# Two chunks of a projection by eight plain products instead of seven Winograd products, in an encoder block on one core

## The chip, the core and the metric

The kernel runs on one core of a Trainium2 chip. The core has a matrix engine (PE, with a loader for the stationary operand, PEld), three engines for elementwise work (DVE, ACT and POOL) and SP, which here only issues transfers. Each engine takes its instructions strictly in the order in which the program holds them, and waits for semaphores that other engines and transfers raise. The metric is device time in microseconds from the first to the last instruction of the one core; the median of three runs of the kernel before is 1972.98 us (1972.03 to 1973.51).

## What is computed

One layer of an encoder. `x` has 2048 rows of 1024 features. All that matters here stands at the head of the reference:

```python
h = rms_norm(x, norm_gain[l])
proj = jnp.einsum('bsd,df->bsf', h, w_in[l])
q_a, k_a, v_a, g_a, q_r, k_r, v_r, g_r, m_a, m_r = split_columns(proj)
# chunk_band_attention on q_a, k_a, v_a; retention_chunkwise on q_r, k_r, v_r;
# both gated, projected, merged, projected by w_out, added to x, normalised
```

Inputs and outputs are float32, and a float32 product is made of three passes: every operand is held as a high part (rounded to the engine's format) and a low part (what the rounding left), and high x high, low x high and high x low are summed.

## The kernel before

**Tiling.** The rows come in two passes of 1024 (`s` = 0, 1). In a pass the normalised rows, transposed, are a 2 x 2 matrix of blocks: a11 and a12 are the left and right 512 features of the first 512 rows (`xa` in the code), a21 and a22 those of the next 512 (`xb`). The weights come in chunks of 256 columns, and a chunk is also 2 x 2: b11, b12 (upper features, left and right 128 columns), b21, b22 (lower features). Job `p0` is the first pass over 14 chunks: chunk 0 is q of the attention, chunk 1 its k, chunk 2 the k of the retention (which is then rotated), and so on. After it come the gates (`g0`), the second pass (`p1`, `g1`), and the output projections, with attention and retention woven in between.

**Seven products.** A chunk is made by the Winograd form of Strassen's method (class `Strassen`, L334): seven products instead of eight, of operands that are sums. On the side of the rows seven operands lie resident in R[0] to R[6], as high and low parts: R[0] = a11, R[1] = a12, R[2] = a22, R[3] = s1 = a21 + a22, R[4] = s2 = s1 - a11, R[5] = s3 = a21 - a11, R[6] = s4 = a12 - s2. On the side of the weights POOL makes four differences per chunk, t1 to t4 (`SUMS_OF`, L320, and `sum`, L335; at which product they are made stands in `SUM_AT`, L321). `PRODUCTS` (L227) pairs them; `ORDERS` (L44) gives the order of the seven by the first letter of the job. Each operand of the weights is split by ACT (`wh`, the high part) and DVE (`wl`, the low part) in `make`, L294. The results u2, u3 and c22 are summed by ACT and DVE out of PSUM in `product`, L372, before an epilogue (`ep_qa`, `ep_ka`) splits them again and stores them by SP.

**A product** is 12 matmuls of 128x512 on PE (`matmuls`, L302: four slices of 128 features, three passes), counted as four steps. `run_to(n)` (L529) emits steps until the n-th; `prime(n)` (L457) emits the preparation of the weights for the first n products; `later` puts a piece of work some steps on.

**The front.** At the start nothing is resident. `start_up` (L545) writes out an order by hand: SP loads the rows and the eight quarters of the weights of chunks 0 and 1; ACT and DVE sum the squares and scale the rows; PE transposes them (16 transposes of 128x128 for each of the four blocks, into four PSUM buffers `TR`); `hi` (ACT) and `lo` (DVE) split the transposed blocks into R, `to_parts` the sums. The products of the two chunks stand in between, in the order `FRONT` (L45), by turns for chunk 0 and chunk 1: with R[0], R[1], R[2], R[4], R[5], R[3], R[6]. From chunk 2 on the order "p" holds, and `dense` (L468) emits the products with the preparation three products ahead. `keep_in_program_order` makes every engine keep the order in which the code is written, so an instruction that waits holds back all that stands behind it on its engine.

## Time and profile before

| what | value |
|---|---|
| median of 3 runs | 1972.98 us (1972.03 to 1973.51) |
| the profiled execution: its time, its span | 1975.88 us, 1974.2 us |
| PE busy, share of the span | 1906.4 us, 97% |
| DVE, ACT, POOL busy | 71%, 48%, 50% |
| PE busy in 17 to 32, 32 to 47, 47 to 58, 58 to 70 us | 14.86 of 15, 11.21 of 15, 7.58 of 11, 8.69 of 12 us |
| first matmul of a product; first of chunk 2; first of chunk 3 | 17.16, 78.45, 97.49 us |

How to read it: a row of the timeline gives start, duration, engine, line, operation, the tile written and the tiles read by the program's names without their numbers, the shape, the count of merged instructions, and in brackets how long the engine sat idle just before and what ended that. Nearly all instructions have line 142, where the helper records them, so the tiles tell them apart: `r` is a part of R, `wh_p` and `wl_p` are parts of weights in job p0 or p1, `t_p` a difference of weights, `pa` and `p` are PSUM tiles of transposed rows, `ps_p_x`, `y`, `v`, `z`, `w` the PSUM banks of the Winograd products, `raw_f` and `b` the weights of chunks 0 and 1, `raw_p` those of later chunks. A matmul's duration runs on into the next one, so the step of PE is read from start to start.

### The profile page before, as it was taken

What the parts mean: (1) busy time and instruction counts of PE and PEld (TensorE: products, weight loads), DVE (VectorE), ACT (ScalarE), POOL (GpSimd) and SP (SyncE); (2) the same over time, 40 slices, a digit from 0 to 9 for tenths busy, and PEclk for the clock granted to TensorE, in tenths of its full rate; (3) what the DMA queues carried; (4) which work ended last, traced back from release to release, by engine and by line L of the source; (5) the groups of instructions that cost most, each with busy time, mean ns of one, the idle gap of its engine ahead of it and who ended that gap; (6) DMA issues with size and microseconds to landing.
All of it is one profiled execution on the core that took longest, in us unless ns stands there. A gap on an engine that the chain in (4) does not pass through costs nothing. (4 is left out here: it accounts for less than half of the span.)

```text
span 1974.2 us, 30273 instructions
## 1 busy us (share of the span) xinstructions
PE 1906.4 (97%) x9616; PEld 1586.6 (80%) x9616; DVE 1399.1 (71%) x2567; ACT 938.7 (48%) x1893; POOL 993.1 (50%) x799
## 2 busy tenths in 40 slices
PE   6899999999999999999999999999999999999997
PEld 4677878888888887778887888888888878887886
DVE  7887778677765667988887677766556754557876
ACT  6454554466655454433343555554456322223554
POOL 2343544554556666544544454444566214557775
PEclk9999999999999999999999999999999999999999
DMA  4575796655539996676684745553999899987674
GB/s 150 165 259 183 228 297 207 205 162 170 174 113 283 272 269 234 209 246 196 192 256 161 211 141 163 165 162 102 273 278 296 294 371 332 313 271 244 202 222 142
DMA packets 335054, 434.84 MB, mean 220 GB/s; under 512 B 30040, under 2 KB 194544, under 8 KB 334896
## 3 DMA queue, kind: packets, MB, share of 16 engines
q1 hardware_dynamic: 269152, 368.42, 58.8%
q10 hardware_dynamic: 65744, 64.50, 10.7%
q8 instruction: 77, 1.26, 0.3%
q14 instruction: 81, 0.66, 0.1%
HBM read 288.21 MB, written 144.60 MB: 219 GB/s over the span
## 5 line engine op out<-in xcount | busy, mean ns | idle before, releaser
L142 POOL TENSOR_SCALAR pr<-pr,rsum 128x640 f32<-128x640 f32 (+4 forms) x128 | 96.0, 750 | 226.6 <-DVE ptl L142 108.3
L142 POOL TENSOR_TENSOR t_p<-raw_p,t_p 128x512 f32<-128x512 f32 x50 | 74.2, 1484 | 148.8 <-DVE wl_p L142 131.1
L142 PE MATMUL ps_p_z<-r,wh_p 128*128 128x512 f32 x448 | 141.4, 397 | 5.5 <-DVE c_p L142 2.8
L142 PE MATMUL ps_g_z<-r,wh_g 128*128 128x512 f32 x448 | 144.2, 403 | 2.0 <-DVE c_g L142 1.9
L142 DVE CUSTOM_DVE_ANT_0 pr<-wide,bt 128x640 f32<-128x640 f32 (+4 forms) x128 | 94.3, 737 | 71.6 <-PE wide L142 62.5
L142 PE MATMUL ps_g_x<-r,wh_g 128*128 128x512 f32 x448 | 142.9, 400 | 0.7 <-ACT u_g L142 0.7
L142 PE MATMUL ps_p_x<-r,wh_p 128*128 128x512 f32 x448 | 141.7, 397 | 1.4 <-ACT u_p L142 1.4
L142 ACT ACTIVATE pr<-pr,mn 128x640 f32<-128x640 f32 (+4 forms) x128 | 98.0, 765 | 84.9 <-DVE mn L142 84.9
L142 DVE TENSOR_TENSOR ptl<-tp,pth 128x384 fp32r<-128x384 f32 x168 | 95.9, 573 | 41.1 <-ACT pth L142 40.6
L142 ACT CAST pth<-tp 128x384 fp32r<-128x384 f32 x168 | 84.6, 515 | 70.9 <-PE tp L142 65.3
L142 POOL TENSOR_TENSOR sl<-sm,sh 128x512 fp32r<-128x512 f32 x64 | 89.4, 1397 | 57.3 <-ACT sh L142 30.9
L142 DVE TENSOR_TENSOR wl_p<-t_p,wh_p 128x512 fp32r<-128x512 f32 x112 | 105.9, 947 | 1.9 <-ACT wh_p L142 1.9
L142 DVE TENSOR_TENSOR sm<-sr,dm 128x512 f32<-128x512 f32 x64 | 44.1, 689 | 79.1 <-PE sr L142 35.2
L142 PEld LDWEIGHTS ps_p_z<-r,wh_p 128*128 128x128 f32 x448 | 81.7, 188 | 22.7 <-issue 5.5
L142 PEld LDWEIGHTS ps_p_x<-r,wh_p 128*128 128x128 f32 x448 | 83.4, 190 | 19.7 <-ACT u_p L142 2.2
L142 PE MATMUL wide<-ka,qa 128*128 128x512 f32 (+2 forms) x448 | 94.7, 327 | 2.3 <-DVE mn L142 2.3
L142 POOL TENSOR_TENSOR wl_g<-t_g,wh_g 128x512 fp32r<-128x512 f32 x56 | 75.3, 1345 | 41.4 <-ACT wh_g L142 31.4
L142 PEld LDWEIGHTS tp<-ident,pr 128*128 128x128 f32 x560 | 71.3, 141 | 27.5 <-POOL pr L142 2.2
L142 PE MATMUL po<-pth,va 128*128 128x256 f32 x336 | 92.8, 297 | 0.0
L142 ACT CAST wh_p<-t_p 128x512 fp32r<-128x512 f32 x112 | 69.1, 619 | 49.0 <-PE ps_p_z L142 22.5
L142 PE MATMUL tp<-ident,pr 128*128 128x128 f32 x560 | 89.0, 273 | 2.9 <-POOL pr L142 1.6
L142 PEld LDWEIGHTS wide<-ka,qa 128*128 128x128 f32 x448 | 75.5, 189 | 19.5 <-DVE mn L142 7.7
(885 smaller groups left out, 6023.7 us busy)
## 6 DMA issues: line engine op xcount, KB each, us to landing
raw_g<-in_w_in_dram ACTq DMA_DIRECT2D x56, 512.0 KB, 5.3
raw_p<-in_w_in_dram ACTq DMA_DIRECT2D x50, 512.0 KB, 6.1
qa<-qas SPq DMA_DIRECT2D x128, 128.0 KB, 3.0
qr<-qrs SPq DMA_DIRECT2D x128, 128.0 KB, 4.7
vr<-vrs SPq DMA_DIRECT2D x64, 256.0 KB, 5.6
ka<-kas SPq DMA_DIRECT2D x40, 256.0 KB, 3.7
va<-vas SPq DMA_DIRECT2D x40, 256.0 KB, 3.1
kds<-kdt_k SPq DMA_DIRECT2D x32, 256.0 KB, 4.8
```

Of the source, the lines that this page charges most:

```text
L142: return tc.keep_in_program_order(op(*a, **k))
```

## The change

Chunks 0 and 1 of job p0 are made by the eight plain products a(i,j) x b(j,h), class `Front`, without t1 to t4 and without u2, u3 and c22: the two products with j = 0 and j = 1 add up in one PSUM bank, and the epilogue reads the bank. The order is i, then j, then the chunk, then h: the first eight products need only a11 and a12, the next four a21, the last four a22. a21 is held in R[6] until the twelfth product is done, and the parts of the weights, which are used twice, lie in R[5] (b11, b12) and R[3] (b21, b22) until the twelfth and the sixteenth. Sums s1 to s4 are made beside the products; s4 = a12 - s2 goes from DVE to POOL. The third chunk uses order "h": R[0], R[2], R[4], R[5], R[3], R[1], R[6], with t1, t2, t3 made before its first product and t4 before its second. The loads of the weights' quarters stand earlier on SP, between the rows of the first and the second block, and the loads of chunk 2 earlier on ACT. `second_half`, which prepares the second pass, is given 8 steps instead of 24, counted from a place that is 24 steps later.

```diff
-FRONT = (0, 3, 5, 1, 2, 4, 6)
+ORDERS["h"] = (0, 5, 1, 2, 4, 3, 6)
...
+        "h": {0: ("t1", "t2", "t3"), 5: ("t4",)},
...
+    class Front(Chunk):
+        def prepare(self, n):
+            i, j, c = n
+            if i:
+                return
+            m, slot = (5, 3)[j], 2 * self.c + c
+            ws = [R[m][part][:, slot, :].rearrange("p (k c) -> p k c", k=4) for part in range(2)]
+            src = self.b[f"b{j + 1}{c + 1}"]
+            act.copy(ws[0], src)
+            dve.tensor_tensor(ws[1], src, r32(ws[0]), ALU.subtract)
+            self.parts[j, c] = ws
+        def product(self, n):
+            i, j, c = n
+            o = self.bank((i, c))
+            yield from self.matmuls(o, self.parts[j, c], R[((0, 1), (6, 2))[i][j]], j == 0, j == 1)
+            if j:
+                self.job.epilogue(self.c, i, c, o, True)
...
+            kind = lambda c: Plain if resident else Front if name == "p0" and c < front else Strassen
...
+            if name == "p0":
+                self.orders[front] = "h"
...
+                seq[:0] = [(c, n) for n in LAST for c in range(front)] if name == "p1" else [
+                    (c, (i, j, h)) for i in range(2) for j in range(2) for c in range(front) for h in range(2)
+                ]
...
         prime(2)
+        run_to(4)
         a11 = [E(f"a11_{k}") for k in range(4)]
...
-        run_to(4)
-        prime(3)
+        prime(4)
+        run_to(8)
         ps = [TR(f"pa1_{k}") for k in range(4)]
...
+        run_to(16)
+        for f in (0, 1):
+            for t in range(4):
+                scale(xb, "b", t, f, t % 2)
+        prime(8)
...
+        run_to(24)
+        ps = [TR(f"p21_{k}") for k in range(4)]
...
+            hi(6, k, ps[k], k)
+            lo(6, k, ps[k], k)
+            if k == 1:
+                run_to(28)
+        run_to(32)
...
+        for k in range(4):
+            dve.scalar_tensor_tensor(s2[k], ps[k], ng[:, 4 + k:5 + k], s3[k], ALU.mult, ALU.add)
+            pool.tensor_tensor(s4[k], a12[k], s2[k], ALU.subtract)
...
-    second_half(24)
+    second_half(8)
```

**On PE, at the start.** `pa` with a number are the transposed rows, `ps_p_0_x` the first bank of chunk 0; `r_81` and `r_82` are the parts of R[0], `r_91` and `r_92` of R[5]. Before, behind the last matmuls of the first product:

```order
L142 MATMUL ps_p_0_x<-r_81,wh_p_0_0_537 128x512
L142 MATMUL ps_p_0_x<-r_82,wh_p_0_0_537 128x512
L142 MATMUL ps_p_0_x<-r_81,wl_p_0_0_538 128x512
L142 MATMUL pa_0_608<-ident,xa_1_454 128x128
L142 MATMUL pa_0_608<-ident,xa_1_456 128x128
```

and with the change:

```order
L142 MATMUL ps_p_0_(0, 0)_586<-r_81,r_91 128x512
L142 MATMUL ps_p_0_(0, 0)_586<-r_82,r_91 128x512
L142 MATMUL ps_p_0_(0, 0)_586<-r_81,r_92 128x512
L142 MATMUL ps_p_0_(0, 1)_611<-r_81,r_91 128x512
L142 MATMUL ps_p_0_(0, 1)_611<-r_82,r_91 128x512
```

A second product with R[0] now stands ahead of the transposes of the right half of `xa`.

**On POOL, its first work.** `t_p_0`, `t_p_1` and `t_p_2` are the differences of weights of chunks 0, 1 and 2, `a_0_672` to `a_3_675` the tiles of a12, `a_0_599` to `a_3_602` those of s2. Before:

```order
L142 TENSOR_TENSOR t_p_0_717<-raw_f_471 128x512
L142 TENSOR_TENSOR t_p_0_719<-raw_f_472,t_p_0_717 128x512
L142 TENSOR_TENSOR t_p_0_721<-raw_f_472,t_p_0_719 128x512
L142 TENSOR_TENSOR t_p_1_800<-raw_f_473 128x512
L142 TENSOR_TENSOR t_p_1_802<-b_641,t_p_1_800 128x512
L142 TENSOR_TENSOR t_p_1_804<-b_640,t_p_1_802 128x512
L142 TENSOR_TENSOR t_p_0_865<-raw_f_471,raw_f_472 128x512
L142 TENSOR_TENSOR t_p_1_867<-raw_f_473,b_641 128x512
```

and with the change:

```order
L142 TENSOR_TENSOR a_0_672<-a_0_672,a_0_599 128x512
L142 TENSOR_TENSOR a_1_673<-a_1_673,a_1_600 128x512
L142 TENSOR_TENSOR a_2_674<-a_2_674,a_2_601 128x512
L142 TENSOR_TENSOR a_3_675<-a_3_675,a_3_602 128x512
L142 TENSOR_TENSOR t_p_2_958<-raw_p_2_0_750 128x512
L142 TENSOR_TENSOR t_p_2_960<-raw_p_2_1_816,t_p_2_958 128x512
L142 TENSOR_TENSOR t_p_2_962<-raw_p_2_0_750,raw_p_2_1_816 128x512
L142 TENSOR_TENSOR t_p_2_992<-raw_p_2_1_816,t_p_2_960 128x512
```

The eight differences for chunks 0 and 1 are gone; s4 has come, and t4 of chunk 2 is POOL's eighth operation.

**On ACT, behind that t4.** `t_p_2_992` is t4 of chunk 2, `r_93` is the high part of R[6] and `r_87` that of R[3], `ps_p_1` the banks of chunk 1. With the change:

```order
L142 CAST wh_p_2_5_994<-t_p_2_992 128x512
L142 CAST r_93<-a_0_672 128x512
L142 CAST r_93<-a_1_673 128x512
L142 DMA raw_p_3_0_1002<-in_w_in_dram 128x4x256
L142 CAST h_ka_0_1018<-ps_p_1_(1, 0)_896 128x512
L142 CAST r_93<-a_2_674 128x512
L142 CAST r_93<-a_3_675 128x512
L142 DMA raw_p_3_1_1026<-in_w_in_dram 128x4x256
L142 CAST h_ka_1_1042<-ps_p_1_(1, 1)_909 128x512
L142 CAST wh_p_2_1_1046<-t_p_2_960 128x512
L142 CAST r_87<-a_0_818 128x512
```

Before, the high part of chunk 2's second product was that of t1, not of t4, and no cast of R stood behind it:

```order
L142 CAST wh_p_2_0_1015<-raw_p_2_0_952 128x512
L142 CAST h_ka_1_1037<-c_p_1_1033 128x512
L142 CAST h_ka_0_1040<-u_p_1_979 128x512
L142 DMA raw_p_3_0_1043<-in_w_in_dram 128x4x256
L142 CAST wh_p_2_4_1047<-t_p_2_1011 128x512
```

ACT's cast of R[6] and R[3] now stands behind a wait for POOL.

More of the change, by code (lines that the diff above doesn't have):

```diff
@@ L356, in sums @@
                 self.b = {f"b{j + 1}{c + 1}": self.half(j, c) for j in range(2) for c in range(2)}
-            if self.c < self.job.front and self.job.name == "p0":
-                return
             for s in SUMS_OF:
                 if s[0] in SUM_AT[self.job.orders[self.c] if strict[0] else "loose"].get(n, ()):
-                    early = self.c >= self.job.front or self.c == 0 and s[0] != "t4"
+                    early = (self.c >= self.job.front or self.c == 0 and s[0] != "t4") and (
+                        self.job.orders[self.c] != "h" or s[0] != "t3")
                     self.sum(*s, None if early else E)
@@ L435, in __init__ @@
             self.lead = 1 if not resident else kh
-            self.chunks = [(Plain if resident else Strassen)(self, c) for c in range(n)]
+            kind = lambda c: Plain if resident else Front if name == "p0" and c < front else Strassen
+            self.chunks = [kind(c)(self, c) for c in range(n)]
             per = range(4 * kh) if resident else ORDERS[name[0]]
@@ L446, in __init__ @@
             if front:
-                seq[:0] = [(c, n) for n in (LAST if name == "p1" else FRONT) for c in range(front)]
+                seq[:0] = [(c, n) for n in LAST for c in range(front)] if name == "p1" else [
+                    (c, (i, j, h)) for i in range(2) for j in range(2) for c in range(front) for h in range(2)
+                ]
                 if name == "p1":
@@ L602, in lo @@
             )
+        for i in range(2):
+            ch[1].b[f"b2{i + 1}"] = E(f"b2{i + 1}", shape=(P, 4, P))
         for t in range(4):
             rows(xa, 0, t)
-        quarter(0, "b11")
+        for c in range(2):
+            quarter(c, "b11")
+            quarter(c, "b12")
         rows(xb, B, 0)
         rows(xb, B, 1)
-        quarter(1, "b11")
-        quarter(0, "b21")
-        rows(xb, B, 2)
+        for c in range(2):
+            quarter(c, "b21")
+            quarter(c, "b22")
+            rows(xb, B, 2 + c)
         ps = [TR(f"pa0_{k}") for k in range(4)]
@@ L642, in start_up @@
             turn(ps[k], k, xa, 1)
+        squares(xb, "b", 2, True)
+        squares(xb, "b", 3)
+        chain("b", 0, 4)
+        for k in range(4):
             hi(1, k, ps[k], 4 + k)
             lo(1, k, ps[k], 4 + k)
+        prime(6)
         a12 = [E(f"a12_{k}") for k in range(4)]
-        for i in range(2):
-            ch[1].b[f"b2{i + 1}"] = E(f"b2{i + 1}", shape=(P, 4, P))
-        quarter(1, "b21")
-        rows(xb, B, 3)
-        for c in range(2):
-            quarter(c, "b12")
-            quarter(c, "b22")
@@ L653, in start_up @@
-        run_to(8)
-        prime(4)
-        a21 = [E(f"a21_{k}") for k in range(4)]
-        squares(xb, "b", 3)
-        squares(xb, "b", 2, True)
-        tiny = ACC("tiny")
-        nn["b"][1] = tiny[:, 0:4]
-        chain("b", 0, 4)
+        run_to(16)
[3 more added lines that the diff above has]
+        prime(8)
         for k in range(4):
             act.activation(a12[k], ps[k], AF.Copy, scale=ng[:, 4 + k:5 + k])
-        for f in (1, 0):
-            for t in range(4):
-                scale(xb, "b", t, f, t % 2)
@@ L666, in start_up @@
-        run_to(12)
-        for dst in (0, 1, 3):
-            ch[0].sum(*SUMS_OF[dst])
-        prime(5)
-        run_to(16)
-        p22 = [TR(f"p22_{k}") for k in range(4)]
-        p21 = {}
-        def other(k):
-            p21[k] = ACC(f"p21_{k}")
-            turn(p21[k], k, xb, 0)
-        for k in range(4):
-            turn(p22[k], k, xb, 1)
-            hi(2, k, p22[k], 4 + k)
-            lo(2, k, p22[k], 4 + k)
-        s3 = [E(f"s3_{k}") for k in range(4)]
-        s2 = a11
-        def combine(k):
-            g, g2 = ng[:, k:k + 1], ng[:, 4 + k:5 + k]
-            act.activation(a21[k], p21[k], AF.Copy, scale=g)
-            dve.scalar_tensor_tensor(s3[k], p21[k], g, a11[k], ALU.mult, ALU.subtract)
-            dve.scalar_tensor_tensor(s2[k], p22[k], g2, s3[k], ALU.mult, ALU.add)
@@ L692, in start_up @@
-        other(0)
-        other(1)
-        run_to(20)
-        for dst in (0, 1, 3):
-            ch[1].sum(*SUMS_OF[dst], E)
-        prime(6)
-        combine(0)
-        combine(1)
-        other(2)
-        other(3)
-        to_parts(4, 0, s2[0])
-        to_parts(4, 1, s2[1])
-        prime(7)
-        for k in (2, 3):
-            combine(k)
-            to_parts(4, k, s2[k])
-        run_to(24)
-        prime(8)
-        for c in range(2):
-            ch[c].sum(*SUMS_OF[2], E)
-        prime(9)
+        run_to(24)
@@ new lines, in start_up @@
+        ps = [TR(f"p21_{k}") for k in range(4)]
+        for k in range(4):
+            turn(ps[k], k, xb, 0)
+        for k in range(4):
+            hi(6, k, ps[k], k)
[3 more added lines that the diff above has]
+        run_to(32)
+        a21 = [E(f"a21_{k}") for k in range(4)]
+        s3 = [E(f"s3_{k}") for k in range(4)]
+        for k in range(4):
+            act.activation(a21[k], ps[k], AF.Copy, scale=ng[:, k:k + 1])
+            dve.scalar_tensor_tensor(s3[k], ps[k], ng[:, k:k + 1], a11[k], ALU.mult, ALU.subtract)
@@ new lines, in start_up @@
+        run_to(36)
+        ps = [TR(f"p22_{k}") for k in range(4)]
+        for k in range(4):
+            turn(ps[k], k, xb, 1)
+        for k in range(4):
+            hi(2, k, ps[k], 4 + k)
+            lo(2, k, ps[k], 4 + k)
+        run_to(48)
+        s2, s1, s4 = a11, a21, a12
+        for k in range(4):
+            dve.scalar_tensor_tensor(s2[k], ps[k], ng[:, 4 + k:5 + k], s3[k], ALU.mult, ALU.add)
+            pool.tensor_tensor(s4[k], a12[k], s2[k], ALU.subtract)
+        for k in range(4):
+            dve.scalar_tensor_tensor(s1[k], ps[k], ng[:, 4 + k:5 + k], a21[k], ALU.mult, ALU.add)
+            to_parts(4, k, s2[k])
@@ L713, in start_up @@
+        run_to(52)
+        prime(17)
         for k in range(4):
             to_parts(5, k, s3[k])
-        s1 = a21
-        for k in range(4):
-            dve.scalar_tensor_tensor(s1[k], p22[k], ng[:, 4 + k:5 + k], a21[k], ALU.mult, ALU.add)
-        prime(10)
-        run_to(32)
-        prime(11)
+        run_to(56)
+        prime(18)
+        for k in range(2):
+            to_parts(6, k, s4[k])
+        run_to(60)
+        for k in range(2, 4):
+            to_parts(6, k, s4[k])
+        run_to(64)
@@ L721, in start_up @@
+        prime(19)
         for k in range(4):
             to_parts(3, k, s1[k])
-        prime(12)
-        for k in range(4):
-            dve.tensor_tensor(s2[k], a12[k], s2[k], ALU.subtract)
-        run_to(36)
-        prime(13)
-        for k in range(4):
-            to_parts(6, k, s2[k])
-        run_to(40)
-        prime(14)
     def second_half(at):
@@ L1072, in projection @@
                 kind = "k" if col == C_KR else "q"
-                for n, i in ((4, 1), (5, 0)):
+                for n, i in ((4, 1), (5, 0)) if (name, c) != ("p0", front) else ((5, 1), (2, 0)):
                     hooks[name, c, n] = [lambda a=(kind, cc, 2 * s + i): load_tables(*a)]
@@ L1747, in hybrid_kernel @@
         for i in range(2):
-            hook(j.name, i, 1 if j is jobs[2] else 2, lambda j=j, i=i: j.chunks[2].load([i]))
+            hook(j.name, i, 1 if j is jobs[2] else (0, 1, 1), lambda j=j, i=i: j.chunks[2].load([i]))
     start_up()
```

## The prediction

> **What bounds the kernel now.** I read the page first, then the windows by stage, then PE's timeline of the first 100 us.

> ```profile
> span 1974.2 us, 30273 instructions
> PE 1906.4 (97%) x9616; PEld 1586.6 (80%) x9616; DVE 1399.1 (71%) x2567; ACT 938.7 (48%) x1893; POOL 993.1 (50%) x799
> PE   6899999999999999999999999999999999999997
> ```

> PE sets the time. Its slices are full but for the first two and the last: of the 67.8 us in which PE is not busy, a large part lies at the start. The windows (us from the start; per engine busy us and instructions, then the granted clock, DMA share, GB/s) and PE's own timeline there:

> ```profile
> 17.00:32.00 15.00, 14.86 (x65) 11.62 (x64) 12.45 (x28) 12.74 (x25) 5.89 (x4) 1.00 0.33 87
> 32.00:47.00 15.00, 11.21 (x59) 8.44 (x60) 13.38 (x23) 10.37 (x18) 5.41 (x4) 1.00 0.25 71
> 47.00:58.00 11.00, 7.58 (x23) 4.91 (x21) 9.60 (x16) 8.26 (x15) 0.00 (x0) 0.84 0.00 0
> 58.00:70.00 12.00, 8.69 (x36) 6.60 (x36) 12.00 (x21) 4.30 (x8) 6.22 (x2) 1.00 0.26 87
> 17.16:97.49 80.33, 69.49 (x300) 54.19 (x301) 68.86 (x115) 47.29 (x87) 26.91 (x16) 0.98 0.43 125
> ```

> ```profile
> 17.16 1.58 PE L142 MATMUL ps_p_x<-r,wh_p 128*128 128x512 f32 x2
> ...
> 21.81 1.91 PE L142 MATMUL pa<-ident,xa 128*128 128x128 f32 x16
> 23.48 0.71 PE L142 MATMUL ps_p_x<-r,wh_p 128*128 128x512 f32 x2
> ...
> 32.92 3.27 PE L142 MATMUL p<-ident,xb 128*128 128x128 f32 x24 [1.02 <-DVE xb L142]
> ...
> 50.64 0.50 PE L142 MATMUL ps_p_y<-r,wh_p 128*128 128x512 f32 x1 [1.37 <-ACT r L142]
> ...
> 52.38 1.05 PE L142 MATMUL ps_p_y<-r,wh_p 128*128 128x512 f32 x2
> ...
> 53.66 1.05 PE L142 MATMUL ps_p_y<-r,wh_p 128*128 128x512 f32 x2
> ...
> 58.90 0.70 PE L142 MATMUL ps_p_v<-r,wh_p 128*128 128x512 f32 x2 [2.50 <-DVE u_p L142]
> ...
> 66.12 0.69 PE L142 MATMUL ps_p_z<-r,wh_p 128*128 128x512 f32 x2 [1.53 <-ACT r L142]
> ...
> 70.21 0.70 PE L142 MATMUL ps_p_z<-r,wh_p 128*128 128x512 f32 x2 [1.09 <-DVE u_p L142]
> ...
> 78.45 0.62 PE L142 MATMUL ps_p_x<-r,wh_p 128*128 128x512 f32 x2
> ...
> 81.17 0.62 PE L142 MATMUL ps_p_z<-r,wh_p 128*128 128x512 f32 x2
> ...
> 97.49 0.61 PE L142 MATMUL ps_p_x<-r,wh_p 128*128 128x512 f32 x2
> ```

> Up to 32 us PE is full, on a11 and a12 alone. From 32 to 70 us it waits, and the waits end on DVE and ACT: they make the sums of rows (`r`) and the results (`u_p`) there, and DVE is busy 12.00 of 12 us. From 70.21 PE runs through. A product costs 81.17 - 78.45 = 2.72 us, so chunk 2 (seven products, 19.04 us) starts at 78.45 and chunk 3 at 97.49. The 16 transposes of a block cost 23.48 - 21.81 = 1.67 us. The first product takes 21.81 - 17.16 = 4.65 us, 1.93 above its price, at a slow step; between 52.38 and 53.66 three matmuls take 1.28 us where 0.68 is usual, and the clock of that window is 0.84.

> **The change part by part.** PE's matmuls first: 24 are added (two products, 5.44 us), everything else on PE is the same work in another order. If PE never waited between its first product and chunk 3, it would need 23 products x 2.72 = 62.56, three blocks of transposes 5.01, the slow first product 1.93: 69.5 us against the 80.33 of the window above. The most that can be won is so 10.8 us, net of the two products. What is left to find is how much PE waits, and I follow the handoffs by the steps of these rows (DVE, then ACT). All times of the changed kernel below are estimates added up from them:

> ```profile
> 20.58 1.13 DVE L142 TENSOR_TENSOR wl_p<-raw_f,wh_p 128x512 fp32r<-128x512 f32 x1
> ...
> 24.68 2.71 DVE L142 SCALAR_TENSOR_TENSOR r<-pa,ng,r 128x512 fp32r<-128x512 f32 x4
> ...
> 28.24 0.68 DVE L142 CUSTOM_DVE_ANT_0 junk<-xb 128x512 bf16<-128x512 f32 x1
> ...
> 29.66 0.16 DVE L142 SCALAR_TENSOR_TENSOR n_b<-ss_b 128x4 f32<-128x4 f32 x1
> ...
> 32.28 1.68 DVE L142 TENSOR_SCALAR xb<-xb,n_b 128x512 f32<-128x512 f32 x4
> ...
> 58.07 1.28 DVE L142 TENSOR_TENSOR u_p<-ps_p_y,u_p 128x512 f32<-128x512 f32 x2
> ...
> 62.88 2.49 DVE L142 TENSOR_TENSOR a<-a,a 128x512 f32<-128x512 f32 x4
> ...
> 103.46 1.78 DVE L142 TENSOR_TENSOR wl_p<-t_p,wh_p 128x512 fp32r<-128x512 f32 x1
> ```

> ```profile
> 19.23 2.44 ACT L142 ACTIVATE a<-pa,ng 128x512 f32<-128x512 f32 x4
> ...
> 23.01 2.42 ACT L142 ACTIVATE r<-pa,ng 128x512 fp32r<-128x512 f32 x4
> ...
> 50.49 1.13 ACT L142 CAST wh_p<-t_p 128x512 fp32r<-128x512 f32 x2
> ```

> So a low part or a sum on DVE steps at 0.62 (SBUF) to 0.68 us (PSUM), a group of four at 2.5 to 2.7; on ACT a cast at 0.57, a group of four at 2.4.

> *Removed.* Ten sums u2, u3, c22 on DVE and two copies on ACT (6.4 and 1.1 us), six low and six high parts of weights (3.7 and 3.4 us), the four subtractions of s4 on DVE (2.5 us), eight differences on POOL. *Added.* Four high and four low parts of a21 in R[6] (2.4 and 2.7 us), s4 on POOL. DVE loses 16 operations net, about 9.9 us, ACT and POOL four each. In the 58 to 70 window, where DVE is full, that load is what PE waits for.

> *Products 1 to 8 (a11, a12).* Product 1 as before, 17.16 to 21.81. Product 2 needs one more low part of weights, where DVE stood at 20.58 with an operation of its own: ready by 21.2 to 21.7, no wait. Transposes of a12 to 26.2, products 3 and 4 to 31.64. Product 5 needs R[1] and b21. ACT is through with a11, two casts and two sums of squares by 24, DVE with two low parts by 23.5, two squares of `xb` (28.24 to 29.66, 1.42) by 24.9, the chain of the norm (29.66 to 32.28, 2.62) by 27.5, four low parts of R[1] by 30.2, that of b21 by 30.9. It is due at 31.64, for its third matmul at 32.1: 1.2 us to spare, the thinnest place of the first half. Products 5 and 6 end at 37.1; `xb` is scaled by 33 (1.68 a group of four); its left half is transposed to 38.75; products 7 and 8 end at 44.2.

> *Products 9 to 12 (a21 in R[6]).* ACT's third and fourth high part stand behind the epilogue of product 7, which can't start before 41.5; they are made by 43.3, the last low part by 44.4, due at 46.2. The right half of `xb` is then due at 46.9, and its four PSUM buffers come free with s3 on DVE: the fourth at 48.2, when PE wants it at 48.17. I charge 0.3 us. The buffers of two tiles of s3 were those of stores:

> ```profile
> qas<-h_qa SPq DMA_DIRECT2D x1, 256.0 KB, 2.5
> ```

> On SP's queue these stores stand in the order of the epilogues; the last that matters is issued at about 44.1 and lands at 46.6, where s3 wants the tile at 47.5. Hidden, with 0.9 us to spare. Product 12 ends at 56.9.

> *Products 13 to 16 (a22) and chunk 2.* R[2] is ready by 51 and due at 56.9. Then DVE makes s2, s1 and the low parts of R[4] (12 operations, about 8 us) to 59 to 61.5, R[5]'s by 64 to 65. Chunk 2 is due at 67.8 and its first part is ready by 63. Its second product is due at 70.5 and needs t4, POOL's eighth operation from 51.7 on:

> ```profile
> 19.87 1.29 POOL L142 TENSOR_TENSOR t_p<-raw_f 128x512 f32<-128x512 f32 x1 [18.57 <-DMA raw_f<-in_w_in_dram]
> ...
> 61.28 5.22 POOL L142 TENSOR_TENSOR t_p<-raw_p 128x512 f32<-128x512 f32 x1 [17.52 <-DMA raw_p<-in_w_in_dram]
> ```

> ```profile
> L142 POOL TENSOR_TENSOR t_p<-raw_p,t_p 128x512 f32<-128x512 f32 x50 | 74.2, 1484 | 148.8 <-DVE wl_p L142 131.1
> ```

> At 1.29 each t4 is there at 62. But beside each other the two engines delay each other: the same low part takes DVE 0.62 alone, 1.13 at 20.58 beside POOL's row at 19.87, 1.78 at 103.46, and POOL's row at 61.28 lasts 5.22 us, through all of DVE's `a<-a,a` at 62.88. If DVE and POOL alternate, POOL needs about 1.9 an operation and t4 is there at 67; if POOL is shut out while DVE makes R[5], at 68.3, and with ACT's cast and DVE's low part the product has its operands at 69.5. Still in time by 1 us. But behind that cast on ACT stand R[6], two epilogues, the loads of chunk 3 and the high part of the third product: 4.3 us to 73.1, its low part 73.8, due at 73.65. I charge 0.3, and 0.2 for the fourth. R[3], free at 67.8, is ready by 76 and due at 78.6. Chunk 3's second product is due at 90; its low part stands on DVE behind ten operations that can start at 81.5 and end by 88.6: nothing, or 1 us if one of them meets POOL. I charge 0.2.

> [...]

> The sum: 10.8 - 0.3 - 0.5 - 0.2 = 9.8 us, so chunk 3 would start at 87.7. From 78.45 on PE hardly waited, and so the shift should carry to the end: the span would be 1974.2 - 9.8 = 1964.4. The profiled execution (1975.88 around its span) is 2.9 us above the median of the runs; taken off the median, **1963.2 us**. Unknown are the waits: from none (10.8 won, 1962.2) to 3 us more than charged (1966.2).

> One term rests on the clock. The slow stretch at 52 us follows a wait of 1.37 us and cost some 1.6 us (half rate for about 3.3 us); I count it as won, since PE has no such wait now. [...]

> **The rivals.** *(A) Forecast*, PE nearly dense: 1961.5 to 1966.

> *(B) The first half comes too early for the rows.* The second block's rows now stand behind three more quarters of weights on SP, and the norm and R[1] hang on the last of them. For it: 1.2 us to spare only. Against it: the transfers are the same 24. At 4 us late PE waits 3 us more and again for a21: 5 to 7 us are left, 1966 to 1968.

> *(C) The win is given back within the pass.* PE's later waits:

> ```profile
> PE pst L142 <- ACT xs L142: 2.9, 5, 1.1
> PE ps_p_z L142 <- DVE c_p L142: 1.6, 2, 1.2
> ```

> If DVE, not PE, set the pace of the chunks behind, PE would only wait longer there: about 1972.5. Against it: these waits are 4.5 us from 100 to 300 us, and DVE comes 9.9 us lighter, as much as PE gains.

> *(D) Slower: POOL is shut out.* If every one of POOL's eight operations took the 5.22 of the row at 61.28, t4 would come at 51.7 + 41.8 = 93.5, PE would stand still from 70.5 to 94.6, 24 us, and the kernel would take about 1973 - 10.8 + 24 = 1986. It turns slower when t4 comes after some 80, that is at more than 3.5 us an operation; waits begin at 2.2. For it: DVE runs without a pause from 51 to 76. Against it: about half of its operations there read PSUM, and over the whole kernel 50 such differences take 1484 ns each in the mean (the page's group above).

> That the change doesn't do what it says can be left out: the order on PE, ACT and POOL shows it.

> **How the numbers follow.** A 0.76, B 0.11, C 0.08, D 0.05. What a measurement can tell is about 0.2%, 4 us: faster means under 1969.0. A and nearly all of B are faster, C is the same, D slower: 0.87, 0.08, 0.05. The range takes A with a little for later waits that vanish, and B: 1961.0 to 1968.0; A's own is 1961.5 to 1966.

> **What would show it.** Chunk 3's first matmul at 87 to 88.5 (the first `ps_p_x` after chunk 2), against 97.49. PE busy at 14.5 or more of 15 us from 32 to 47. POOL's `t_p` of chunk 2 done by 68, and no wait of PE above 1 us from 17 to 90. Wrong would be a wait before `ps_p` with R[1] at 31.6 (B), a wait on `wh_p` at 70.5 (D), or chunk 3 in time and the span not shorter (C).

## The result: 1962.1 us, 0.57% faster

The changed kernel takes 1962.13 us in the median of 8 runs (1959.70 to 1971.52), the kernel before 1974.04 us in 8 runs beside them: a ratio of 0.9943 (95% interval 0.9931 to 0.9955). Five more runs of the changed kernel on another occasion gave 1961.38 us against 1974.02, a ratio of 0.9935 (0.9920 to 0.9950). The forecast was 1963.2 us, 9.8 us won from a median of 1972.98 us; measured are 11.9 and 12.6 us won.

The head of the page after, and the same four windows as before (per engine busy us and instructions, then granted clock, DMA share, GB/s):

```profile
span 1957.6 us, 30307 instructions
PE 1904.1 (97%) x9640; PEld 1589.9 (81%) x9640; DVE 1393.9 (71%) x2551; ACT 936.0 (48%) x1889; POOL 982.5 (50%) x795
PE   7999999999999999999999999999999999999997
```

```profile
17.00:32.00 15.00, 14.96 (x68) 12.17 (x68) 13.50 (x34) 14.04 (x28) 0.00 (x0) 1.00 0.31 96
32.00:47.00 15.00, 15.00 (x77) 12.60 (x76) 8.54 (x15) 8.89 (x16) 0.00 (x0) 1.00 0.55 153
47.00:58.00 11.00, 10.97 (x57) 9.08 (x56) 11.00 (x16) 5.08 (x9) 6.31 (x5) 1.00 0.22 79
58.00:70.00 12.00, 12.00 (x55) 9.94 (x54) 11.33 (x15) 8.76 (x17) 7.63 (x5) 1.00 0.55 176
```

PE is full in all four windows; before it was busy for 11.21 of 15, 7.58 of 11 and 8.69 of 12 us in the last three. DVE's share fell from 13.38 to 8.54 of 15 us in 32 to 47 us, but in 47 to 70 us it is as full as before. PE's own timeline shows where chunk 2 and chunk 3 start, and the first wait of any size behind them:

```profile
67.91 0.62 PE L142 MATMUL ps_p_x<-r,wh_p 128*128 128x512 f32 x2
...
87.04 0.61 PE L142 MATMUL ps_p_x<-r,wh_p 128*128 128x512 f32 x2
...
105.68 0.63 PE L142 MATMUL trva<-ident,c_p 128*128 128x128 f32 x4 [0.77 <-DVE c_p L142]
```

Chunk 3 starts at 87.04 us instead of 97.49: 10.45 us of the possible 10.8 are won in the front. Between chunk 3's start and the first matmul of the gates lies the same work in both kernels. One window over that stretch, first of the kernel before, then of the changed one:

```profile
97.49:339.63 242.14, 235.69 (x1109) 190.91 (x1108) 191.77 (x274) 122.80 (x275) 105.82 (x73) 1.00 0.73 238
```

```profile
87.04:328.00 240.96, 235.37 (x1110) 191.09 (x1108) 190.48 (x273) 123.10 (x275) 106.10 (x73) 1.00 0.73 237
```

It is 1.2 us shorter (and 240.84 us in a second trace of the changed kernel): nothing is given back, a little more is won, and where in this stretch was not taken apart. Together 11.6 us, close to the 11.9 and 12.6 us of the medians. The two profiled executions lie 16.6 us apart in span; the other 5 us come behind the gates, where all the kernels of this study do the same work, and where their traces take from 1628.3 to 1640.2 us (before 1634.6, after 1629.6). Most of that part is scatter of single executions: the profiled one of the kernel before lies 1.8 us above its median (1975.88 us), that of the changed kernel 2.4 us below (1959.70 us).

### The profile page after: what moved, and what is told of

It reads as the page before. It is cut to its first block, busy times and chain, and to the rows that moved or that the text cites. A ratio compares the mean times of both kernels' runs of the same rounds, so it can differ in the third digit from the quotient of the medians.

```text
span 1957.6 us, 30307 instructions
## 1 busy us (share of the span) xinstructions
PE 1904.1 (97%) x9640; PEld 1589.9 (81%) x9640; DVE 1393.9 (71%) x2551; ACT 936.0 (48%) x1889; POOL 982.5 (50%) x795
## 3 DMA queue, kind: packets, MB, share of 16 engines
q10 hardware_dynamic: 65744, 64.50, 10.8%
## 5 line engine op out<-in xcount | busy, mean ns | idle before, releaser
L142 POOL TENSOR_SCALAR pr<-pr,rsum 128x640 f32<-128x640 f32 (+4 forms) x128 | 96.0, 750 | 226.3 <-DVE ptl L142 108.3
L142 POOL TENSOR_TENSOR t_p<-raw_p,t_p 128x512 f32<-128x512 f32 x50 | 74.0, 1480 | 142.9 <-DVE wl_p L142 129.1
L142 PE MATMUL ps_g_z<-r,wh_g 128*128 128x512 f32 x448 | 143.3, 401 | 2.2 <-DVE c_g L142 2.2
L142 DVE CUSTOM_DVE_ANT_0 pr<-wide,bt 128x640 f32<-128x640 f32 (+4 forms) x128 | 94.3, 737 | 71.6 <-PE wide L142 62.9
L142 PE MATMUL ps_g_x<-r,wh_g 128*128 128x512 f32 x448 | 143.0, 400 | 0.7 <-ACT u_g L142 0.7
L142 ACT ACTIVATE pr<-pr,mn 128x640 f32<-128x640 f32 (+4 forms) x128 | 98.0, 765 | 84.8 <-DVE mn L142 84.8
L142 PE MATMUL ps_p_z<-r,wh_p 128*128 128x512 f32 x416 | 131.5, 397 | 3.1 <-DVE c_p L142 3.1
L142 PE MATMUL ps_p_x<-r,wh_p 128*128 128x512 f32 x416 | 130.1, 394 | 1.5 <-ACT u_p L142 1.5
L142 DVE TENSOR_TENSOR ptl<-tp,pth 128x384 fp32r<-128x384 f32 x168 | 95.9, 573 | 40.7 <-ACT pth L142 40.3
L142 ACT CAST pth<-tp 128x384 fp32r<-128x384 f32 x168 | 84.6, 515 | 70.5 <-PE tp L142 66.7
L142 POOL TENSOR_TENSOR sl<-sm,sh 128x512 fp32r<-128x512 f32 x64 | 88.6, 1384 | 53.9 <-ACT sh L142 26.0
L142 DVE TENSOR_TENSOR wl_p<-t_p,wh_p 128x512 fp32r<-128x512 f32 x104 | 96.8, 932 | 2.1 <-ACT wh_p L142 2.1
L142 DVE TENSOR_TENSOR sm<-sr,dm 128x512 f32<-128x512 f32 x64 | 44.1, 688 | 75.2 <-PE sr L142 37.4
L142 PE MATMUL wide<-ka,qa 128*128 128x512 f32 (+2 forms) x448 | 94.7, 327 | 2.1 <-DVE mn L142 2.1
L142 POOL TENSOR_TENSOR wl_g<-t_g,wh_g 128x512 fp32r<-128x512 f32 x56 | 75.2, 1342 | 41.4 <-ACT wh_g L142 40.2
L142 PEld LDWEIGHTS tp<-ident,pr 128*128 128x128 f32 x560 | 71.3, 141 | 27.4 <-POOL pr L142 2.2
L142 PE MATMUL po<-pth,va 128*128 128x256 f32 x336 | 92.9, 297 | 0.0
L142 PE MATMUL tp<-ident,pr 128*128 128x128 f32 x560 | 89.0, 273 | 2.9 <-POOL pr L142 1.6
L142 PEld LDWEIGHTS wide<-ka,qa 128*128 128x128 f32 x448 | 75.5, 189 | 19.2 <-DVE mn L142 7.3
L142 PEld LDWEIGHTS ps_p_x<-r,wh_p 128*128 128x128 f32 x416 | 76.9, 188 | 17.5 <-ACT u_p L142 2.4
L142 PEld LDWEIGHTS ps_p_z<-r,wh_p 128*128 128x128 f32 x416 | 75.9, 188 | 18.3 <-issue 4.3
L142 PE MATMUL po<-ptl,va 128*128 128x256 f32 x336 | 88.4, 285 | 1.1 <-DVE ptl L142 0.2
## 6 DMA issues: line engine op xcount, KB each, us to landing
vr<-vrs SPq DMA_DIRECT2D x64, 256.0 KB, 5.3
ka<-kas SPq DMA_DIRECT2D x40, 256.0 KB, 3.6
va<-vas SPq DMA_DIRECT2D x40, 256.0 KB, 3.1
kds<-kdt_k SPq DMA_DIRECT2D x32, 256.0 KB, 4.1
```

The lines of the kernel that those rows point to most:

```text
L142: return tc.keep_in_program_order(op(*a, **k))
```

## The experiments

Each kernel has a trace, so each is read twice: by chunk 3's start, which is exact to a few tenths, and by its time, whose single runs spread over 2.5 to 12 us for one kernel. The kernel before was run beside each set; its medians there were 1974.04 us, 1975.5 (ten sums less, order p, ten sums late, POOL), 1975.3 (R[1], ten sums early, s4, 24 steps) and 1974.02 (the last set), so that times of different sets differ by up to 1.5 us for that reason alone. One part of chunk 3's start is chance too: the first matmuls of the first product step at 0.42 us in place of 0.23, and it takes 4.16 to 4.97 us from trace to trace (4.36 in the changed kernel; 5.64 behind the transposes of the unit matrix). "Net" below is the time from the end of the first product to chunk 3, against that of the changed kernel. "Chunk 3" and "gates" are the starts of their first matmuls; all in us:

| kernel | chunk 3 | net | gates | gates to the end | median (runs) |
|---|---|---|---|---|---|
| before | 97.49 | | 339.63 | 1634.6 | 1974.04 (8) |
| changed | 87.04 | 0 | 328.00 | 1629.6 | 1962.13 (8) |
| changed, again | 86.84 | -0.1 | 327.68 | 1628.3 | 1961.38 (5) |
| before without ten sums | 91.87 | | 333.41 | 1630.5 | 1971.48 (10) |
| chunk 2 in order p | 89.02 | 2.0 | 330.52 | 1631.3 | 1963.96 (3) |
| ten sums more, late | 90.06 | 2.7 | 331.04 | 1630.8 | 1964.41 (3) |
| POOL eight more | 97.23 | 9.7 | 338.92 | 1636.2 | 1973.88 (8) |
| R[1] late | 89.07 | 2.4 | 330.41 | 1631.6 | 1964.13 (4) |
| ten sums more, early | 89.94 | 2.2 | 331.95 | 1632.2 | 1967.19 (7) |
| s4 on DVE | 86.69 | -0.1 | 328.18 | 1633.4 | 1961.17 (4) |
| 24 steps | 86.86 | 0.0 | 322.95 | 1632.6 | 1957.56 (4) |
| 24 steps, again | 86.89 | -0.1 | 322.93 | 1631.7 | 1957.90 (6) |
| transposes of the unit matrix | 88.50 | | 328.64 | 1637.4 | 1967.08 (5) |
| three edits together | 86.91 | | 323.01 | 1640.2 | 1960.51 (6) |

**How much is DVE's load alone?** The kernel before, with the sums of chunks 0 and 1 taken away:

```diff
-                dve.tensor_tensor(self.u2, ps["y"], self.u2, ALU.add)
+                bare or dve.tensor_tensor(self.u2, ps["y"], self.u2, ALU.add)
...
-                dve.tensor_tensor(c22, ps["z"], self.u3, ALU.add)
+                act.copy(c22, ps["z"]) if bare else dve.tensor_tensor(c22, ps["z"], self.u3, ALU.add)
```

> The kernel before, with the ten sums u2, u3 and c22 of chunks 0 and 1 taken off DVE; six of them are ACT copies of the last bank instead, four are left out, so the results of these two chunks are not the reference's. PE's order stays as before. It asks how much of the 10.45 us by which chunk 3 starts earlier (97.49 to 87.04) comes from the lighter DVE alone. Theory: DVE was late in 52 to 70 us, but PE also waited for R[4] and R[5], which need a21 and a22; chunk 3 starts at 92 to 94 us, 4 to 5 us won, time 4 to 5 us under the kernel before. Rival, only DVE's load counts: 87 to 88. Rival, only the order of the operands counts: 97.

Measured: chunk 3 at 91.87 us, 5.6 of the 10.45 us. The windows of this kernel show which part that is:

```profile
32.00:47.00 15.00, 10.71 (x57) 8.07 (x58) 13.42 (x23) 10.38 (x18) 5.41 (x4) 1.00 0.25 71
47.00:58.00 11.00, 9.33 (x31) 6.57 (x32) 9.59 (x16) 7.81 (x14) 0.00 (x0) 0.84 0.00 0
58.00:70.00 12.00, 12.00 (x55) 9.94 (x54) 12.00 (x22) 8.91 (x18) 8.13 (x1) 1.00 0.35 110
```

From 58 us on PE is full without the sums: the three waits of 2.50, 1.53 and 1.09 us are gone. Up to 51 us PE waits for operands of the second block as before, and a stretch of low clock stands behind that as before (0.84 from 47 to 58 us). So a little over half comes from ten sums less on DVE, and the rival by which only the order counts falls. The other 4.8 us come with the rest of the change: two products more that need the first block only, and what else it takes off DVE, six low parts of weights above all. This run does not part these two; that it is the order is argued from PE's waits for the second block up to 51 us, and not shown. The time fell by less than chunk 3's start promised (a ratio of 0.9977, interval 0.9967 to 0.9988, some 4.5 us against the 1975.5 us beside it), though the gates start 6.2 us earlier; what is lost behind them is open.

**The order of chunk 2.**

```diff
-            if name == "p0":
-                self.orders[front] = "h"
...
-                for n, i in ((4, 1), (5, 0)) if (name, c) != ("p0", front) else ((5, 1), (2, 0)):
+                for n, i in ((4, 1), (5, 0)):
```

The second hunk puts the loads of the rotation's tables back to the products where they stand in order p.

> The changed kernel with chunk 2 in the order p (R[0], R[3], R[1], R[2], R[4], ...) in place of h. Theory: R[3] can only be made when its slot is free of b21 and b22 at 67.9 us, and then takes DVE and ACT until about 75.7; chunk 2's second product, due at 70.6, waits for it 4 to 5 us, chunk 3 starts at 91 to 92, and the time is 4 to 5 us above the changed kernel (1966 to 1967). Rival, PE has other cover there and the order is of no weight: chunk 3 at 87 and 1962.

Measured: 2.0 us, less than half of what was expected. PE's rows at chunk 2's second product, which now is that with R[3]:

```profile
71.78 0.50 PE L142 MATMUL ps_p_z<-r,wh_p 128*128 128x512 f32 x1 [0.81 <-DVE r L142]
...
73.48 0.50 PE L142 MATMUL ps_p_z<-r,wh_p 128*128 128x512 f32 x1 [0.73 <-DVE r L142]
...
89.02 0.62 PE L142 MATMUL ps_p_x<-r,wh_p 128*128 128x512 f32 x2
```

The product does not wait for the whole of R[3]: it takes its four slices one after the other, and so runs beside DVE, which makes them one after the other. I had charged the wait to the last slice and not to each by itself. The order is of weight, but 2 us of it.

**Sums put back, late and early.** Ten sums of a bank and a tile, in the second and in the first half of the front:

```diff
             if j:
                 self.job.epilogue(self.c, i, c, o, True)
+            if j and i == 1:
+                for _ in range(3 - c):
+                    dve.tensor_tensor(C("dum"), o, r32(R[0][0][:, 0, :]), ALU.add)
```

(and with `i == 0`).

> The changed kernel with ten sums of a PSUM bank and a tile in SBUF put back on DVE, behind products 13 to 16 and the two before (those with j = 1 of the second half: three for each bank of chunk 0, two for each of chunk 1); nothing reads what they make. About 6.5 us more on DVE between 54 and 70 us, where it has 11.33 of 12 us in use. Theory: DVE's load there sets R[5], the low part of t4 and R[3]; chunk 3 starts 3 to 5 us later, at 90 to 92. Rival, PE's slack (t4 is ready 6 us ahead) takes it: 87 to 88.

> The changed kernel with the same ten sums put back on DVE as in the late case, but behind the products of the first half with j = 1 (5 to 8), at 35 to 46 us, where DVE has 8.54 of 15 us in use. Theory: mostly hidden, but the sums behind products 7 and 8 stand ahead of the low parts of R[6] (due 46.2, ready 44.4 by the steps): chunk 3 0.5 to 2 us later, 87.5 to 89. Rival, what counts is DVE's load as a whole, wherever it lies: 90 to 92 as in the late case.

Measured: 2.7 us late, 2.2 us early, net. PE's wait of the late case and the row of DVE that ends it:

```profile
76.49 0.50 PE L142 MATMUL ps_p_y<-r,wl_p 128*128 128x512 f32 x1 [2.20 <-DVE wl_p L142]
```

```profile
75.75 0.68 DVE L142 TENSOR_TENSOR wl_p<-t_p,wh_p 128x512 fp32r<-128x512 f32 x1
```

It is the low part for chunk 2's third product, made at 71.62 us in the changed kernel. PE did not wait for R[5] nor for t4, of which the expectation spoke first. In the early case PE's wait stands elsewhere:

```profile
49.32 2.60 PE L142 MATMUL p<-ident,xb 128*128 128x128 f32 x16 [1.62 <-DVE s L142]
```

These are the transposes of the right half of the second block; their buffers come free with s3. So DVE's load costs PE where a thin place stands behind it, even where DVE has nearly half of its time free, as in 32 to 47 us. The early case came out dearer than its range: the sums stand ahead of R[6] and s3 in DVE's program order, and idle time elsewhere in the window does not help them. By the size of the loss alone the rival of that run, that DVE's load counts wherever it lies, is not told apart (2.2 against 2.7 us); against it speak the places, since in each case PE waits once and for one thing.

**POOL made late.** Eight subtractions more on POOL between s4 and chunk 2's differences:

```diff
+        dum = C("dum")
+        for _ in range(8):
+            pool.tensor_tensor(dum, r32(R[0][0][:, 0, :]), r32(R[0][1][:, 0, :]), ALU.subtract)
```

> The changed kernel with eight more subtractions on POOL before s4 (nothing reads what they make), which hold up t4 of chunk 2. In the changed kernel eight such operations took 12.3 us (51.69 to 64.02) and t4 was there 6 us before PE asks for its product at 70.6. If each takes 1.5 us as there, t4 comes at 76 and PE waits 5 to 7 us at chunk 2's second product: chunk 3 at 92 to 94. If POOL's new operations run while DVE reads PSUM and take 1.29 each, 2 us less. Rival, POOL is shut out once DVE runs (5 us an operation): t4 beyond 90, PE waits 20 us or more.

POOL's rows, PE's wait, and three windows of 3.41 us:

```profile
58.12 13.32 POOL L142 TENSOR_TENSOR dum<-r,r 128x512 f32<-128x512 f32 x8
...
75.15 1.25 POOL L142 TENSOR_TENSOR t_p<-raw_p,t_p 128x512 f32<-128x512 f32 x1
```

```profile
77.10 1.22 PE L142 MATMUL ps_p_w<-r,wh_p 128*128 128x512 f32 x2 [5.79 <-ACT wh_p L142]
...
82.39 0.62 PE L142 MATMUL ps_p_y<-r,wh_p 128*128 128x512 f32 x2
...
86.64 0.50 PE L142 MATMUL ps_p_v<-r,wl_p 128*128 128x512 f32 x1 [0.88 <-DVE wl_p L142]
```

```profile
72.14:75.55 3.41, 0.00 (x0) 0.00 (x0) 0.00 (x0) 0.00 (x0) 3.33 (x4) 1.00 0.21 74
75.55:78.96 3.41, 1.86 (x4) 1.45 (x5) 1.88 (x4) 2.53 (x5) 0.85 (x1) 0.50 0.39 108
78.96:82.38 3.42, 3.42 (x9) 2.64 (x8) 3.42 (x6) 3.42 (x8) 1.75 (x1) 0.50 1.04 337
```

t4 ended at 76.40, and PE waited 5.79 us: both as the theory had it, and the rival of a POOL that is shut out falls, since the eight took 1.67 us each. But chunk 3 came at 97.23, beyond the 92 to 94. From 75.55 us on, in that wait, the clock was granted at 0.50 for 6.83 us; the product took 5.29 us (77.10 to 82.39) instead of 2.72, and a second wait of 0.88 us followed. A wait of 5.8 us cost 9.7. With that the whole gain is gone: 1973.88 us, a ratio of 0.9994 (0.9980 to 1.0008).

**R[1] made late.** Five subtractions on DVE ahead of R[1]'s low parts:

```diff
         chain("b", 0, 4)
+        dum = C("dum")
+        for _ in range(5):
+            dve.tensor_tensor(dum, r32(R[0][0][:, 0, :]), r32(R[0][1][:, 0, :]), ALU.subtract)
```

> The changed kernel with five more subtractions on DVE (nothing reads them) between the norm of the second block and the low parts of R[1]: these and b21's low part come some 3.1 us later (0.62 each). In the changed kernel the last low part of R[1] is there at 29.7 and b21's and b22's at 30.9, with PE due at 32.1. Theory: 1 us of it is slack, PE waits 2 us before product 5; behind it PE has slack or not by R[6] and R[2], so chunk 3 starts at 88.5 to 90. Rival, the slack is larger than the steps said: 87.

```profile
33.73 2.56 PE L142 MATMUL ps_p_(0, 0)_586<-r,r 128*128 128x512 f32 x10 [2.07 <-DVE r L142]
```

```profile
26.85 3.59 DVE L142 TENSOR_TENSOR dum<-r,r 128x512 f32<-128x512 f32 x5
```

In the changed kernel the low parts of b21 and b22 end at 30.93:

```profile
27.02 2.72 DVE L142 SCALAR_TENSOR_TENSOR r<-pa,ng,r 128x512 fp32r<-128x512 f32 x4
29.65 1.28 DVE L142 TENSOR_TENSOR r<-raw_f,r 128x512 fp32r<-128x512 f32 x2
```

The five took 3.5 us, and PE lost 2.4 us net: the slack at product 5 is 1.1 us, and of what goes beyond it everything arrives at chunk 3.

**s4 on DVE.**

```diff
-            pool.tensor_tensor(s4[k], a12[k], s2[k], ALU.subtract)
+            dve.tensor_tensor(s4[k], a12[k], s2[k], ALU.subtract)
```

> The changed kernel with s4 on DVE again in place of POOL: DVE has 2.5 us more from 51 us on, POOL four operations less, so t4 of chunk 2 is there some 6 us earlier. Theory: DVE is full from 47 to 79 us and R[5]'s low parts are what stands nearest to PE, so chunk 3 starts 0 to 2 us later (87 to 89). Rival, POOL was the engine that mattered (t4): 86.7, 0.4 us earlier.

Measured: no difference (-0.1 us net; the 0.35 us at chunk 3 are nearly all the first product's, so that the 86.7 us of the rival were met by chance). t4 was there at 52.6 us in place of 64.0, and PE gained nothing by it. DVE has four operations more, and its next low parts still come no later, 66.46 against 66.90 for that of t4. The rows of DVE here say why:

```profile
51.29 1.83 DVE L142 TENSOR_TENSOR a<-a,a 128x512 f32<-128x512 f32 x1
...
56.60 0.69 DVE L142 TENSOR_TENSOR a<-a,a 128x512 f32<-128x512 f32 x1
...
57.87 0.68 DVE L142 TENSOR_TENSOR r<-a,r 128x512 fp32r<-128x512 f32 x1
...
63.45 2.49 DVE L142 TENSOR_TENSOR r<-s,r 128x512 fp32r<-128x512 f32 x4
```

and in the changed kernel, with s4 on POOL, DVE's and then POOL's:

```profile
57.08 1.12 DVE L142 TENSOR_TENSOR r<-a,r 128x512 fp32r<-128x512 f32 x1
...
61.19 1.68 DVE L142 TENSOR_TENSOR wl_p<-raw_p,wh_p 128x512 fp32r<-128x512 f32 x1
62.79 3.59 DVE L142 TENSOR_TENSOR r<-s,r 128x512 fp32r<-128x512 f32 x4
...
66.90 0.67 DVE L142 TENSOR_TENSOR wl_p<-t_p,wh_p 128x512 fp32r<-128x512 f32 x1
...
71.62 0.68 DVE L142 TENSOR_TENSOR wl_p<-t_p,wh_p 128x512 fp32r<-128x512 f32 x1
```

```profile
51.69 5.96 POOL L142 TENSOR_TENSOR a<-a,a 128x512 f32<-128x512 f32 x4 [50.39 <-DVE a L142]
...
62.27 1.75 POOL L142 TENSOR_TENSOR t_p<-raw_p,t_p 128x512 f32<-128x512 f32 x1
```

On DVE s4 costs 1.83 and three times 0.69, 3.9 us. On POOL it costs DVE in delay: three low parts of R[4] 1.12 or 1.13 in place of 0.68 (1.3), R[5]'s group 3.59 in place of 2.49 (1.1), a low part of weights 1.68 in place of 0.68 (1.0), 3.4 us in all. The move relieved DVE by half a microsecond and not by the 2.5 us that I took off its load. Over the whole kernel DVE's busy time fell by 5.2 us (1399.1 to 1393.9), where I had counted 9.9.

**When the second pass is prepared.** The changed kernel starts `second_half` 8 steps on, which is the same place against the chunks as 24 steps were before.

```diff
-    second_half(8)
+    second_half(24)
```

> The changed kernel with the preparation of the second pass at 24 steps, as before, in place of 8. Chunk 3's start stays at 87.0. Theory: the time is that of the changed kernel within 2 us; what the profiled pair shows behind 100 us beyond the 10.5 us of the front (6 us) is chance from run to run, and chunk 3's start to the end differs by as much here. Rival, the earlier preparation of the second pass is a part of the gain: 3 to 6 us above the changed kernel.

This was meant to show chance alone, and showed a gain instead: 1957.56 us. It was run once more beside the changed kernel:

> The changed kernel with the second pass prepared from 24 steps on in place of 8, once more, to part its 4.6 us from chance. Theory: PE's waits at the transposes for the second pass (about 2.3 us between 180 and 256 us, and more at 166 to 175 and 235 to 238 us) come from pieces that fall together with the rotation and the transposes of v; 16 steps later they miss each other; the first matmul of the gates again at 322.9 in place of 328.0 us, and the time 3 to 5 us under the changed kernel in the same call. Rival, chance: within 1.5 us of it.

> The changed kernel unaltered, beside the others on the same chip: chunk 3 at 87.0, 1960 to 1964 us. By the run of the kernel before and by chance of the half-rate stretches behind the front its time from chunk 3 on should lie at 1860 to 1865 us.

(From chunk 3 to the end of the span it is 1869.2 us here and 1870.6 in the first trace, not 1860 to 1865; that was off.) 1957.90 against 1961.38 us; over both occasions 10 runs of the one have a median of 1957.6, 13 runs of the other 1961.5. Against the kernel before it is 0.9920 (0.9903 to 0.9938). The window from chunk 3 to the gates, to be held against the 240.96 us above, and the two waits of the list of waits in it, of the changed kernel and of this one:

```profile
86.89:322.93 236.04, 232.67 (x1109) 191.11 (x1108) 192.84 (x273) 123.36 (x279) 106.61 (x72) 1.00 0.74 244
```

```profile
PE pst L142 <- ACT xs L142: 2.3, 5, 0.6
PE ps_p_z L142 <- DVE c_p L142: 1.8, 2, 1.2
```

```profile
PE pst L142 <- ACT xs L142: 2.1, 2, 1.6
...
PE ps_p_z L142 <- DVE c_p L142: 0.4, 1, 0.4
```

The same matmuls take 4.9 us less, in both traces. The wait for `c_p`, the results that DVE adds up, fell from 1.8 to 0.4 us; `pst`, the transposes for the second pass, wait less often but as long in all. Matmul by matmul the two traces run alike up to 166 us; the lead arises between there and 317 us, where the transposes for the second pass stand (179.4 to 295.9 us in the changed kernel, 189.7 to 302.6 in this one). So the expectation of the second run holds for the time and the place. That it is pieces which no longer meet is not shown, and which of DVE's or ACT's they would be is open. This version is faster than both kernels.

**Transposes of the unit matrix at the start.**

```diff
+        for n in range(WARM[0]):
+            pe.transpose(ps[n % 4][:, 0:P], ident, ident)
...
+                for n in range(WARM[1]):
+                    pe.transpose(ps[n % 4][:, 2 * P:3 * P], ident, ident)
```

> The changed kernel with 62 transposes of the unit matrix that nothing reads, on PE ahead of the first transposes of rows and between the two groups of them. In the changed kernel the clock is recorded at full rate from 20.0 us only, and until then a matmul steps at 0.42 us in place of 0.23. [...] But product 5 has only 1.0 us of slack (R[1]'s low parts, as the case with these late showed), so PE waits 1 to 1.6 us there and chunk 3 starts at 85.8 to 86.4, about 1 us earlier. [...] Rival, the rate does not depend on PE's work: 87.

```profile
14.88 1.27 PE L143 MATMUL pa<-ident,xa 128*128 128x128 f32 x8 [1.38 <-DVE xa L143]
16.97 5.85 PE L143 MATMUL ps_p_(0, 0)_648<-r,r 128*128 128x512 f32 x12 [0.81 <-ACT r L143]
```

```profile
13.08:16.50 3.42, 1.69 (x12) 1.06 (x10) 2.56 (x11) 2.10 (x6) 0.00 (x0) 1.00 1.11 349
16.50:19.91 3.41, 2.94 (x6) 2.03 (x7) 3.30 (x8) 3.41 (x7) 0.00 (x0) 0.50 1.12 330
```

Neither the 85.8 to 86.4 us nor the rival's 87 came. The transposes at 15 us were faster, 1.27 in place of 2.05 us. But the first product then waited for ACT's high parts of R[0] and started at 16.97, where it starts at 17.08 in the changed kernel; the clock was granted at 0.50 from 16.50 to 19.91 us and on to 23.3, and the product took 5.64 us. The expected wait before product 5 rested on a lead of PE that no run shows: the first product ended at 22.61 us here, at 21.44 in the changed kernel. Chunk 3 came at 88.50.

**Three edits together.** s4 on DVE, 24 steps and these transposes in one kernel:

> The changed kernel with the three edits that each brought chunk 3 or the gates forward: s4 on DVE, the second pass from 24 steps on, and the 62 transposes of the unit matrix. If they add up: chunk 3 at 85.5 to 86.2 (0.35 for s4, about 1 for the transposes), the gates 5 us earlier on top, 1955 to 1958 us, 4 to 7 us under the changed kernel. Rival: s4 on DVE delays R[6] and R[2] when PE comes earlier, and only the 24 steps are left: 1957 to 1959.

Chunk 3 at 86.91, the gates at 323.01, 1960.51 us: the gates are 5 us earlier, as with the 24 steps alone, the other two edits brought nothing, and the time of this profiled execution was lost behind the gates (1640.2 us, the longest of all). It does not beat the 24 steps alone, and misses the 1957 to 1959 us of its rival too: PE does not wait between 19 and 105 us, so R[6] and R[2] were not late. Behind the gates it is not chance of one execution alone: the median less the start of the gates is 1637.5 us here and 1638.4 with the transposes alone, and 1633.0 to 1635.2 us in all the other versions of the changed kernel. Why these transposes should cost some 3 us there is open.

## Why the prediction was right, point by point

- **The bound of 10.8 us and the dense front.** Right: 10.45 us were won up to chunk 3. PE in 32 to 47 us was to be busy for 14.5 at least and was for 15.00; no wait of 1 us was to stand between 17 and 90 us, and none does.
- **The waits.** Charged were 1.0 us. By the starts of the products PE lost 0.28 us at the transposes of the right half of the second block (charged 0.3), 0.09 in chunk 2's fourth product (charged 0.2), and 0.13 in each of three products behind transposes, which I had not counted: 0.76 in all, and the first product was 0.29 us shorter by chance. The 0.2 for chunk 3's second product was not needed; it stands behind chunk 3's start, so it had no place in the 87.7 either. Nor was the 0.3 for the third product of chunk 2: its low part was made from 71.62 on, 1.5 us before its use, where I had it at 73.8. The step that was off is the chain on ACT behind t4, since t4 came earlier.
- **t4 on POOL.** Bounded by 62 and 68.3, it came at 64.02: eight operations in 12.3 us, 1.54 each. POOL was delayed, but not shut out. No run shows POOL shut out while DVE makes R[5], on which the 68.3 rested and with it the 0.3 us for chunk 2's third product; t4's own operation took 1.75 us (62.27) beside R[5]'s low parts (from 62.79). Waits were to begin at 2.2 us an operation; from the run with POOL late (0.70 us from t4's end to the product, due at 71.1) it is t4 at 70.4, 2.3 us. The point from which rival D makes the kernel slower was set too far, however: not 3.5 us an operation (t4 at 80), but 3.1 (t4 at 76.4 gave the whole gain back), because with that wait of 5.79 us came 6.83 us at a granted clock of 0.50 and a second wait of 0.88 us.
- **The thinnest place, product 5.** Predicted 1.2 us to spare, measured 1.1 by making R[1] late. The low parts of R[1] and of b21 and b22 ended at 30.9 us, as the steps had it for b21. Of rival B the run with R[1] late shows the first wait (rows 3.5 us late cost 2.4), but not the second one, for a21; in the changed kernel nothing made the rows late.
- **DVE's relief.** Off in size: of the 9.9 us taken from DVE the 2.5 for s4 came back as delay by POOL. PE did not feel it: it does not wait there, and the low part of weights behind came 1.5 us before its use.
- **The shift carries to the end (rival C).** Right: from chunk 3 to the gates 1.2 us more were won, none lost. The remaining difference to the forecast, 2.1 to 2.8 us, is 0.65 us more up to chunk 3, these 1.2 us, which the sum left out, and the scatter of the medians. That the time came out within 1.1 us of the 1963.2 us is in part luck: the three runs that it was taken from have a median of 1972.98 us, all eight one of 1974.04.
- **The clock.** The sum was right to count the slow stretch at 52 us as won: the changed kernel was granted 1.00 from 47 to 58 us, where it was 0.84 before.

## What to carry to other kernels

Where an engine is the bound and waits in one stage only, compute what it would need there without any wait, and then look for the two or three handoffs with the least to spare: here added load cost PE time at the transposes of the right half (nothing to spare), at product 5 (1.1 us) and at a low part of weights (1.5 us), and DVE, the engine that looked fullest, took four operations more without a cost. Before moving an operation from DVE to POOL, count what POOL's operation will add to DVE's neighbours: here 3.4 of 3.9 us. And retime background work when the front of a kernel moves: the same place that it had is not the best one, which was worth 3.5 us here.
